# Second product of the second MLP as seven products of half blocks per group, output token-major

## The chip, the cores and the metric

The kernel runs as one program on one core of a Trainium2 chip. The metric is device time in microseconds of one execution. TensorE (PE) multiplies, and its weight loads (PEld) overlap the multiplications; VectorE (DVE) and ScalarE (ACT) work on tiles in SBUF and PSUM; GpSimd (POOL) works on tiles in SBUF; SyncE (SP) issues the DMAs. Each engine takes its own instructions in a fixed order and waits on semaphores.

## The reference

Two residual layers over `x` (1 x 512 tokens x 1024 channels, float32): an attention mixer in the first, an S5 state-space mixer in the second, and behind each of them an MLP. The change is in the second layer's MLP, which ends the program:

```
def sq_relu_mlp(h, w1, w2):
    return jnp.square(jax.nn.relu(h @ w1)) @ w2
...
        x = x + sq_relu_mlp(rms_norm(x, ffn_norm_g[layer]), w_ff1[layer], w_ff2[layer])
```

`w1` is 1024 x 4096 and `w2` is 4096 x 1024. Both products have the same number of multiplications.

## The kernel before

Activations are held channel-major: `xT` is 8 tiles of 128 channels x 512 tokens. Every float32 operand of a large product is split into a rounded high part (type fp32r) and the rest, and one product of two tiles is three matmuls that add up in PSUM: high by high, high by low, low by high (`mm3`, lines 118 to 120 of the profile). A matmul multiplies a 128x128 stationary tile with 512 moving columns.

The class `Mlp` does an MLP in four groups of 1024 hidden channels (`GF` = 8 tiles). In a group, `run` first makes the hidden channels in two halves `c` of four tiles: two weight tiles of 128 x 4 x 512 (`load_w`, L109 the DMA, L112 the high part on ScalarE, L113 the low part on VectorE, in two instructions of 128x1024 each) and 96 matmuls per half. ScalarE and VectorE then take relu and square out of PSUM (L1408, L1409) and split the result into `ahi` and `alo` (L1412, L1413). The group's second product goes over eight output tiles `d`, each with 8 tiles of `w2` as stationary operand and 24 matmuls, so 192 per group. VectorE multiplies the sum in PSUM with the norm's factor `Rb` (L1437) and adds it to `xT` (L1438).

Split weights lie in tiles `whi` and `wlo` of the pool `weights`, which has two buffers of each, for the whole program: a third split can only be written when all matmuls of the first have been done. The raw weights `wraw` have two buffers as well. Sums take turns in six PSUM tiles (`mm6`, names `mm` and `s`). In the last group `emit` writes each finished output tile to HBM, the last one in two halves of 256 tokens.

The order of instructions on each engine comes from a scheduler that runs when the program is built; it keeps the dependencies and may interleave what the code writes one after the other.

Of the kernel before, what the change touches and what calls it, by code (L numbers as in the profile page):

```python
# [9 lines left out]
F32 = mybir.dt.float32  # L10
# [7 lines left out]
P = 128  # L18
S = 512
# [12 lines left out]
def f32(ap):  # L32
    return ap.bitcast(F32)
# [1294 lines left out]
class Mlp:  # L1328
# [38 lines left out]
        T.nc.vector.tensor_scalar(self.Rb, ss, 1.0 / D, EPS, op0=OP.mult, op1=OP.add)  # L1367
        T.nc.vector.reciprocal(self.Rb, self.Rb)

    def run(self, emit=None, during=None, every=0.0, before_last=None, keep=False, halves=False):  # L1370

        T, xT = self.T, self.xT
        nc, tc = T.nc, T.tc
# [4 lines left out]
        with self.ctx if not keep else ExitStack(), tc.tile_pool(name="ffn_a", bufs=1) as pool:  # L1378
# [10 lines left out]
            for g in range(groups):  # L1389
# [30 lines left out]
                for c in range(2):  # L1420
                    W = [T.load_w(self.w2[g * GF * P + kh * 512:g * GF * P + (kh + 1) * 512,
                                          c * 512:(c + 1) * 512]) for kh in range(2)]
                    if last and before_last is not None:
                        with T.behind(nc.sync):
                            before_last(c)
                    for d4 in range(4):
                        d = 4 * c + d4
                        ds_ = slice(d4 * P, (d4 + 1) * P)
                        n = 2 if halves and last and d == KT - 1 else 1
                        for s in (slice(i * S // n, (i + 1) * S // n) for i in range(n)):  # L1430
                            ps = T.mm6()
                            for j in range(GF):
                                hi, lo = W[j // 4]
                                T.mm3(ps[:, s], hi[:, j % 4, ds_], lo[:, j % 4, ds_], ahi[j][:, s], alo[j][:, s],
                                      j == 0, j == GF - 1)

                            ve.tensor_mul(ps[:, s], ps[:, s], self.Rb[:, s])  # L1437
                            ve.tensor_add(xT[:, d, s], xT[:, d, s], ps[:, s])  # L1438
                            pump(5.2 / n)
                            if emit is not None and last:  # L1440
                                emit(d, s)


_INS = ["x", "mix_norm_g", "ffn_norm_g", "w_in", "g_cq", "w_uq", "g_ckv", "w_ukv", "g_qn_mla", "g_kn_mla",
# [11 lines left out]
def trunk(nc, tc, i, out):  # L1456
    with ExitStack() as ctx:
        T = Trunk(tc, ctx)
        gp = T.cpool.tile([P, 31], F32, name="gains")
        T.load_gains = lambda: nc.sync.dma_start(gp, i["gains"])  # L1460
        gmix0, gcq, gckv = gp[:, 0:8], gp[:, 8:10], gp[:, 10:11]
        gains = [gp[:96, 11:12], gp[:96, 12:13], gp[:, 13:14], gp[:, 14:15]]
        gf = gp[:, 15:23], gp[:, 23:31]
        dp = ctx.enter_context(tc.tile_pool(name="dram", bufs=1, space=bass.MemoryType.DRAM))
        T.s5_dram(dp)

        xT, mlp = T.attention(i["xt"], i["w_in"][0], gmix0, gcq, i["w_uq"][0], gckv, i["w_ukv"][0], gains,
                              i["rope"], i["w_o"][0],
                              lambda xT: Mlp(T, xT, gf[0], i["w_ff1"][0], i["w_ff2"][0], "left"))
        mlp.run(emit=lambda d, s: T.s5_emit(xT, d), before_last=lambda c, pool=mlp.pool: T.s5_open(pool, c), keep=True,  # L1470
                during=T.s5_tables(i["s5p"], i["s5b"], i["s5c"], i["s5d"], i["mix_norm_g"][1]), every=6.0)
        mlp = T.s5(xT, i["w_glu"][0],
                   lambda xT: Mlp(T, xT, gf[1], i["w_ff1"][1], i["w_ff2"][1], "right"), mlp.ctx)
        mlp.run(emit=lambda d, s: nc.sync.dma_start(out[d * P:(d + 1) * P, s], xT[:, d, s]), halves=True)


def layout(inputs):
# [24 lines left out]

def unlayout(out):

    return np.ascontiguousarray(out.reshape(D, 8, S // 8).transpose(2, 1, 0)).reshape(1, S, D)


# [14 lines left out]
```

## Time and profile before

| | us |
|---|---|
| median of 3 runs | 1221.34 |
| lowest, highest | 1215.32, 1222.2 |
| profiled execution | 1218.8 |
| its span, first to last instruction | 1217.1 |

The profile shows one execution. Its time beside its span leaves 1.7 us that lie around the instructions. A duration in a row is that of one instruction or of a run of equal ones (x2, x4); instructions of one engine overlap a little at their ends, so the step from one start to the next is shorter than the duration. "Granted clock" is TensorE's clock as a share of 2.4 GHz; 0.5 is 1.2 GHz.

### The profile page before, as it was taken

How to read it: one execution, taken by the hardware profiler on the slowest of the kernel's cores; microseconds unless marked ns; L12 is line 12 of the kernel's file. 1: busy time of each engine (PE TensorE's matmuls, PEld its weight loads, DVE VectorE, ACT ScalarE, POOL GpSimd, SP SyncE). 2: the span in 40 equal slices, each digit the busy share in tenths (PEclk: the TensorE clock that was granted, in tenths of full speed). 3: DMA queues.
4: the chain of work that ended last, by engine and by line, in shares of the span. 5: the costliest groups of instructions: out<-in, count | busy, mean ns of one | idle time of the engine just before them, and what ended most of it. 6: DMA issues, size and time to landing. Idle time of an engine off the chain costs nothing. (4 is left out here: it accounts for less than half of the span.)

```text
span 1217.1 us, 16430 instructions
## 1 busy us (share of the span) xinstructions
PE 1159.6 (95%) x6296; PEld 966.4 (79%) x6296; DVE 782.8 (64%) x1381; ACT 500.6 (41%) x928; POOL 259.6 (21%) x260
## 2 busy tenths in 40 slices
PE   7989999999999888899999788999999999999998
PEld 7978997778888667788888577878788888888887
DVE  7887766758879988797755577453454444444444
ACT  5857775545421433361342255343341331322321
POOL 5461022214000979424200021101000000000000
PEclk9999997999999998999999778999999999999999
DMA  7302202114433376766769677522322332322421
GB/s 222 104 2 53 70 2 69 36 36 160 134 104 103 105 250 190 227 210 198 243 208 394 207 269 256 188 89 85 104 104 70 104 104 69 112 95 69 138 87 52
DMA packets 123758, 161.94 MB, mean 133 GB/s; under 512 B 15648, under 2 KB 72352, under 8 KB 120992
## 3 DMA queue, kind: packets, MB, share of 16 engines
q1 hardware_dynamic: 123680, 160.90, 40.6%
q8 instruction: 49, 0.80, 0.3%
q14 instruction: 29, 0.24, 0.1%
HBM read 133.75 MB, written 35.52 MB: 139 GB/s over the span
## 5 line engine op out<-in xcount | busy, mean ns | idle before, releaser
L112 ACT CAST whi<-wraw 128x1024 fp32r<-128x1024 f32 x132 | 131.9, 1048 | 221.8 <-PE mm L119 123.9
L113 DVE TENSOR_TENSOR wlo<-wraw,whi 128x1024 fp32r<-128x1024 f32 x132 | 169.7, 1315 | 81.1 <-ACT whi L112 80.9
L118 PE MATMUL mm<-xhi,whi 128*128 128x512 f32 x344 | 136.0, 396 | 1.4 <-ACT whi L112 1.4
L118 PE MATMUL mm<-ahi,whi 128*128 128x512 f32 (+1 forms) x352 | 135.0, 386 | 0.3 <-ACT whi L112 0.3
L119 PE MATMUL mm<-xlo,whi 128*128 128x512 f32 x344 | 135.2, 393 | 0.0
L120 PE MATMUL mm<-ahi,wlo 128*128 128x512 f32 (+1 forms) x352 | 134.0, 386 | 1.3 <-DVE wlo L113 1.3
L119 PE MATMUL mm<-alo,whi 128*128 128x512 f32 (+1 forms) x352 | 135.1, 385 | 0.0
L120 PE MATMUL mm<-xhi,wlo 128*128 128x512 f32 x344 | 133.4, 394 | 0.0
L118 PEld LDWEIGHTS mm<-xhi,whi 128*128 128x128 f32 x344 | 64.7, 188 | 16.6 <-ACT whi L112 1.8
L120 PEld LDWEIGHTS mm<-ahi,wlo 128*128 128x128 f32 x352 | 66.1, 188 | 14.7 <-DVE wlo L113 1.7
L118 PEld LDWEIGHTS mm<-ahi,whi 128*128 128x128 f32 x352 | 66.1, 188 | 13.5 <-ACT whi L112 0.6
L119 PEld LDWEIGHTS mm<-alo,whi 128*128 128x128 f32 x352 | 66.2, 188 | 13.1
L120 PEld LDWEIGHTS mm<-xhi,wlo 128*128 128x128 f32 x344 | 64.5, 188 | 14.8 <-issue 0.2
L119 PEld LDWEIGHTS mm<-xlo,whi 128*128 128x128 f32 x344 | 64.7, 188 | 14.4 <-issue 0.2
L1437 DVE TENSOR_TENSOR mm<-mm,bcast 128x512 f32<-128x512 f32 (+1 forms) x44 | 29.8, 684 | 65.4 <-PE mm L120 65.4
L118 PE MATMUL s<-xhi,whi 128*128 128x512 f32 x168 | 66.5, 396 | 0.0
L119 PE MATMUL s<-xlo,whi 128*128 128x512 f32 x168 | 66.5, 396 | 0.0
L120 PE MATMUL s<-ahi,wlo 128*128 128x512 f32 x168 | 66.2, 395 | 0.0
L118 PE MATMUL s<-ahi,whi 128*128 128x512 f32 x168 | 66.1, 395 | 0.0
L120 PE MATMUL s<-xhi,wlo 128*128 128x512 f32 x168 | 66.1, 395 | 0.0
L119 PE MATMUL s<-alo,whi 128*128 128x512 f32 x168 | 65.9, 392 | 0.0
L899 POOL TENSOR_TENSOR W<-PW,B 128x512 f32<-128x512 f32 x16 | 26.4, 1650 | 155.5 <-DVE B L888 141.5
(485 smaller groups left out, 2863.3 us busy)
## 6 DMA issues: line engine op xcount, KB each, us to landing
wraw<-in_w_ff SPq DMA_DIRECT2D x64, 1024.0 KB
dC<-wC SPq DMA_DIRECT2D x16, 512.0 KB
dB<-wB SPq DMA_DIRECT2D x16, 512.0 KB
wraw<-in_w_glu SPq DMA_DIRECT2D x16, 512.0 KB
tT<-dT SPq DMA_DIRECT2D x7, 1024.0 KB
wraw<-in_w_in SPq DMA_DIRECT2D x24, 256.0 KB
tB<-dB SPq DMA_DIRECT2D x6, 1024.0 KB
tC<-dC SPq DMA_DIRECT2D x6, 1024.0 KB
```

Of the source, the lines that this page charges most:

```text
L112: nc.scalar.copy(hi[:, s, :n], raw[:, s, :n])
L113: nc.vector.tensor_sub(lo[:, s, :n], raw[:, s, :n], f32(hi)[:, s, :n])
L118: te.matmul(ps, whi, xhi, start=start, stop=False)
L119: te.matmul(ps, whi, xlo, start=False, stop=False)
L120: self.last = te.matmul(ps, wlo, xhi, start=False, stop=stop).ins
L899: gp.tensor_mul(dst, pw[a][:, :, 1:9, None].to_broadcast(bc), B[a][:, gs][:, :, None, :].to_broadcast(bc))
L1437: ve.tensor_mul(ps[:, s], ps[:, s], self.Rb[:, s])
```

## The change

Only the second MLP changes: `run_seven` takes the place of `run`. Its first product is the same (two halves `c` of 96 matmuls). The hidden channels `p` now hold relu squared times `Rb`, in two VectorE instructions per tile (L1528, L1529 in the changed kernel), and no split of them is made there.

The second product of a group is cut into half blocks. A is 512 tokens x 1024 hidden channels: A11 and A21 are the first and second 256 tokens of the first 512 channels, A12 and A22 of the other 512. B is the group's part of `w2`, 1024 x 1024, in four blocks B11, B12, B21, B22 of 512 x 512. Seven products of 256 x 512 by 512 x 512 take the place of eight, between sums of blocks. On the side of A, VectorE makes S1 = A21 + A22, S2 = S1 - A11, S3 = A11 - A21, S4 = A12 - S2 (L1535, L1541); on the side of B, GpSimd makes T1 = B12 - B11, T2 = B22 - T1, T3 = B22 - B12, T4 = T2 - B21 (L1487). All seven operands of each side are split into high and low parts: those of A by ScalarE and VectorE (L1494, L1495), those of B by ScalarE (L1501) and VectorE, or GpSimd for T1 and T2 (both L1502). The products run in the order B11, T3, T1, T2, T4, B21, B22.

In a product, a 128x128 piece of A is stationary and 512 columns of B move (L1567 to L1569): 24 matmuls for two PSUM tiles of 128 tokens x 512 channels. Each sum over the groups is kept in SBUF (`acc`, two tiles for each of seven products, six of them in the place of `xT`) and added to by VectorE (L1576). The residual `xT` is transposed once by TensorE into four of the sums (L1465). In the last group VectorE combines the seven sums (L1584 to L1590) and the output, now 512 tokens x 1024 channels, is written in nine DMAs, the last two of 128x256.

```diff
+    def run_seven(self, out):
...
+        groups = FF // (GF * P)
+        pairs = [slice(0, 2), slice(2, 4)]
+        with self.ctx, tc.tile_pool(name="ffn_a", bufs=1) as pool:
+            acc = {n: [pool.tile([P, S], F32, name=f"acc{n}{t}") for t in range(2)] for n in (2, 3, 4, 5)}
+            for i, n in enumerate((1, 6, 7)):
+                acc[n] = [xT[:, 2 * i + t] for t in range(2)]
+
+            def residual():
+
+                for n, h, dh in ((5, 1, 1), (3, 0, 1), (2, 0, 0), (4, 1, 0)):
...
+                            pe.transpose(pt[:, k], xT[:, 4 * dh + k, ts], T.ident)
+                        pf = pt.rearrange("p k d -> p (k d)")
+                        if n == 3:
+                            ve.tensor_sub(acc[3][t], pf, acc[5][t])
+                        elif n == 4:
+                            sc.activation(acc[4][t], pf, AF.Copy, scale=-1.0)
+                        else:
+                            sc.copy(acc[n][t], pf)
...
+                for n, fh, dh in (("B11", 0, 0), ("B12", 0, 1), ("B22", 1, 1), ("B21", 1, 0)):
+                    B[n] = pool.tile([P, 4, 512], F32, name=n)
+                    r = (g * GF + 4 * fh) * P
+                    nc.sync.dma_start(B[n], self.w2[r:r + 512, dh * 512:(dh + 1) * 512].rearrange(
+                        "(k p) n -> p k n", p=P))
...
+                B["T3"] = B["B12"]
+                for n, x, y in (("T1", "B12", "B11"), ("T3", "B22", "B12"), ("T2", "B22", "T1"), ("T4", "T2", "B21")):
+                    for s in pairs:
+                        gp.tensor_sub(B[n][:, s], B[x][:, s], B[y][:, s])
+                return B
+
+            def split_a(v):
+                h, l = (pool.tile([P, 4, 256], F32R, name=n, bufs=4) for n in ("ah", "al"))
+                for s in pairs:
+                    x = v(s)
+                    sc.copy(h[:, s], x)
+                    ve.tensor_sub(l[:, s], x, f32(h)[:, s])
+                return h, l
+
+            def split_b(v, eng):
+                hi, lo = T.hi_lo(4)
+                for s in pairs:
+                    sc.copy(hi[:, s], v[:, s])
+                    eng.tensor_sub(lo[:, s], v[:, s], f32(hi)[:, s])
+                return hi, lo
...
+                for c in range(2):
+                    W = self.W0 if g + c == 0 else []
+                    W = W + [self.w1_tile(g, c, kh) for kh in range(len(W), 2)]
+                    if c == 0:
+                        B = sums(g)
...
+                    if g + c == 0:
+                        residual()
+                    for f in range(4):
+                        p = pf[c][:, f]
+                        ve.scalar_tensor_tensor(p, pss[f], 0.0, self.Rb, op0=OP.max, op1=OP.mult)
+                        ve.scalar_tensor_tensor(p, pss[f], 0.0, p, op0=OP.max, op1=OP.mult)
+                    if c == 0:
+                        A["A11"] = split_a(lambda s: a11[:, s])
+
+                        def s3(s):
+                            t = pool.tile([P, 2, 256], F32, name="s3")
+                            ve.tensor_sub(t, a11[:, s], a21[:, s])
+                            return t
+                        A["S3"] = split_a(s3)
...
+                prepare = {
+                    "S1": summed(a21, a21, a22, OP.add),
+                    "S2": summed(a11, a21, a11, OP.subtract),
+                    "A22": lambda s: a22[:, s],
+                    "A12": lambda s: a12[:, s],
+                    "S4": summed(a12, a12, a11, OP.subtract),
+                }
+                order = [(1, "A11", "B11", ve), (7, "S3", "T3", ve), (5, "S1", "T1", gp), (6, "S2", "T2", gp),
+                         (4, "A22", "T4", ve), (2, "A12", "B21", ve), (3, "S4", "B22", ve)]
+                W = {"B11": split_b(B["B11"], ve)}
+                for i, (n, a, b, _) in enumerate(order):
+                    if i < 6:
+                        W[order[i + 1][2]] = split_b(B[order[i + 1][2]], order[i + 1][3])
+                    for _, ahead, _, _ in order[i + 1:i + 3]:
+                        if ahead not in A:
+                            A[ahead] = split_a(prepare[ahead])
+                    (ah, al), (bh, bl) = A[a], W[b]
+                    for t in range(2):
+                        m = 2 if last and i == 6 and t else 1
+                        for cs in (slice(q * S // m, (q + 1) * S // m) for q in range(m)):
+                            ps = T.mm6()[:, cs]
+                            ts = slice(t * P, (t + 1) * P)
+                            for j in range(4):
+                                pe.matmul(ps, ah[:, j, ts], bh[:, j, cs], start=j == 0, stop=False)
+                                pe.matmul(ps, ah[:, j, ts], bl[:, j, cs], start=False, stop=False)
+                                pe.matmul(ps, al[:, j, ts], bh[:, j, cs], start=False, stop=j == 3)
+                            d = acc[n][t][:, cs]
+                            if g == 0 and n in (1, 6, 7):
+                                sc.copy(d, ps)
+                            elif last and n == 4:
+                                ve.tensor_sub(d, d, ps)
+                            else:
+                                ve.tensor_add(d, d, ps)
...
+                    if last and i == 3:
+                        for t in range(2):
+                            a1, a2, a3, a4, a5, a6, a7 = (acc[n][t] for n in range(1, 8))
+                            ve.tensor_add(a6, a1, a6)
+                            ve.tensor_add(a7, a6, a7)
+                            ve.tensor_sub(a4, a7, a4)
+                            ve.tensor_add(a2, a1, a2)
+                            ve.tensor_add(a6, a6, a5)
+                            ve.tensor_add(a3, a6, a3)
+                            ve.tensor_add(a5, a7, a5)
+                            nc.sync.dma_start(out[(2 + t) * P:(3 + t) * P, 512:1024], a5)
...
-        mlp.run(emit=lambda d, s: nc.sync.dma_start(out[d * P:(d + 1) * P, s], xT[:, d, s]), halves=True)
+        mlp.run_seven(out)
...
-    return np.ascontiguousarray(out.reshape(D, 8, S // 8).transpose(2, 1, 0)).reshape(1, S, D)
+    return np.ascontiguousarray(out.reshape(8, S // 8, D).transpose(1, 0, 2)).reshape(1, S, D)
...
-    nc = bacc.Bacc("TRN2", target_bir_lowering=False, num_devices=1)
+    nc = bacc.Bacc("TRN2", target_bir_lowering=False, num_devices=1, dynamic_dma_scratch_size=2048)
...
-    out = nc.dram_tensor("out_0", (D, S), F32, kind="ExternalOutput").ap()
+    out = nc.dram_tensor("out_0", (S, D), F32, kind="ExternalOutput").ap()
```

Three places show how instructions stand now. Row labels of the changed kernel use its own line numbers.

On GpSimd, at the end of the program: the difference of the two orders (T_ is T1, T2 or T4 of a group, B_ a block of `w2`, 8932 to 8934 the first group's, 95.. the second's).

```order
 L1353 TENSOR_TENSOR xacc<-xacc,xsq 128x512 x7
-L1518 UNCONDITIONAL_BRANCH
-L1518 ISA
+L1487 TENSOR_TENSOR T_8932<-B_8926,B_8924 128x1024 x2
+L1487 TENSOR_TENSOR B_8926<-B_8928,B_8926 128x1024
+L1487 TENSOR_TENSOR T_8933<-B_8928,T_8932 128x1024
+L1487 TENSOR_TENSOR B_8926<-B_8928,B_8926 128x1024
+L1487 TENSOR_TENSOR T_8933<-B_8928,T_8932 128x1024
+L1487 TENSOR_TENSOR T_8934<-T_8933,B_8930 128x1024 x2
+L1502 TENSOR_TENSOR wlo<-T_8932,whi 128x1024 x2
+L1487 TENSOR_TENSOR T_9539<-B_9533,B_9531 128x1024 x2
+L1502 TENSOR_TENSOR wlo<-T_8933,whi 128x1024 x2
```

GpSimd had no work in this MLP; now it has twelve instructions of 128x1024 per group, and T1 of the next group (T_9539) stands between the low part of T1 and the low part of T2 of the running one.

On VectorE, before, in the second product of a group:

```order
L113 TENSOR_TENSOR wlo_9864<-wraw_9862,whi_9863 128x1024 x2
L1437 TENSOR_TENSOR mm_9835<-mm_9835,bcast_8393 128x512
L113 TENSOR_TENSOR wlo_9872<-wraw_9870,whi_9871 128x1024
L1438 TENSOR_TENSOR xT_2736<-xT_2736,mm_9835 128x512
L113 TENSOR_TENSOR wlo_9872<-wraw_9870,whi_9871 128x1024
```

The same engine now, in the second group from the second half of T3's low part (al_9811 is the low part of S1, al_9853 of S2, al_9895 of A22; xT holds sums):

```order
L1502 TENSOR_TENSOR wlo_9805<-B12_9533,whi_9804 128x1024
L1529 SCALAR_TENSOR_TENSOR p1_9514<-s_9693,p1_9514 128x512
L1576 TENSOR_TENSOR xT_2736<-xT_2736,s_9818 128x512
L1541 TENSOR_TENSOR p0_9513<-p0_9513 128x2x256
L1495 TENSOR_TENSOR al_9811<-p0_9513,ah_9810 128x512
L1576 TENSOR_TENSOR xT_2736<-xT_2736,mm_9832 128x512
L1541 TENSOR_TENSOR p0_9513<-p0_9513,p1_9514 128x2x256
L1495 TENSOR_TENSOR al_9853<-p0_9513,ah_9852 128x512
L1495 TENSOR_TENSOR al_9895<-p1_9514,ah_9894 128x512 x2
L1541 TENSOR_TENSOR p0_9513<-p0_9513 128x2x256
L1576 TENSOR_TENSOR xT_2736<-xT_2736,mm_9860 128x512
L1495 TENSOR_TENSOR al_9811<-p0_9513,ah_9810 128x512
```

The low part of S1's second half is the last of these rows; seven instructions with both inputs in SBUF stand between it and T3's low part.

On TensorE, before, in the second product of a group:

```order
L120 MATMUL mm_9835<-ahi_9586,wlo_9740 128x512
L118 MATMUL mm_9835<-ahi_9710,whi_9747 128x512
L119 MATMUL mm_9835<-alo_9711,whi_9747 128x512
L120 MATMUL mm_9835<-ahi_9710,wlo_9748 128x512
L118 MATMUL mm_9835<-ahi_9718,whi_9747 128x512
```

The same engine now, in the second group, where the product with T1 (whi_9846) ends and those with T4 (whi_9928) and T2 (whi_9888) go on:

```order
L1569 MATMUL mm_9900<-whi_9846,al_9811 128x512
L1567 MATMUL mm_9900<-whi_9846,ah_9810 128x512
L1568 MATMUL mm_9900<-wlo_9847,ah_9810 128x512
L1569 MATMUL mm_9900<-whi_9846,al_9811 128x512
L1569 MATMUL s_9914<-whi_9846,al_9811 128x512
L1567 MATMUL s_9914<-whi_9846,ah_9810 128x512
L1568 MATMUL s_9914<-wlo_9847,ah_9810 128x512
L1569 MATMUL s_9914<-whi_9846,al_9811 128x512
L1567 MATMUL mm_9982<-whi_9928,ah_9894 128x512
L1567 MATMUL mm_9996<-whi_9928,ah_9894 128x512
L1568 MATMUL s_9940<-wlo_9889,ah_9852 128x512
L1569 MATMUL s_9940<-whi_9888,al_9853 128x512
```

The first of these rows is the 19th matmul of the product with T1 and the first that reads the second half of S1's low part. The products with T2 and T4 are interleaved, and the first matmul with T4 stands right behind the last one with T1, whose buffer T4's high part takes.

## Rows read from the trace of the kernel before

**Rows 1.** The page's first part: busy time, share of the span and instructions by engine

```profile
PE 1159.6 (95%) x6296; PEld 966.4 (79%) x6296; DVE 782.8 (64%) x1381; ACT 500.6 (41%) x928; POOL 259.6 (21%) x260
```

**Rows 2.** Stretches: engines' busy us and count, granted clock, DMA share, GB/s

```profile
core 0: us, PE busy (x) PEld busy (x) DVE busy (x) ACT busy (x) POOL busy (x), PEclk, DMA share, GB/s
860.00:1210.00 350.00, 350.00 (x1531) 285.32 (x1530) 160.38 (x193) 97.27 (x128) 1.30 (x1) 1.00 0.28 93
```

**Rows 3.** Timeline of TensorE in the last group: start us, duration us, instruction

```profile
1205.10 0.39 PE L120 MATMUL mm<-ahi,wlo 128*128 128x512 f32 x1
1205.33 0.39 PE L118 MATMUL mm<-ahi,whi 128*128 128x512 f32 x1
1205.56 0.39 PE L119 MATMUL mm<-alo,whi 128*128 128x512 f32 x1
```

**Rows 4.** Timeline of VectorE at the tail

```profile
1213.52 0.43 DVE L1437 TENSOR_TENSOR mm<-mm,bcast 128x256 f32<-128x256 f32 x1 [1.75 <-PE mm L120]
```

**Rows 5.** Timeline of TensorE: four transposes of 128x128, and the matmul behind them

```profile
514.78 0.63 PE L920 MATMUL pt<-ident,W 128*128 128x128 f32 x4
515.16 0.48 PE L118 MATMUL mm<-xhi,whi 128*128 128x512 f32 x1
```

**Rows 6.** Timeline of ScalarE in the last group

```profile
1147.50 1.99 ACT L112 CAST whi<-wraw 128x1024 fp32r<-128x1024 f32 x2
1149.39 0.62 ACT L1412 CAST ahi<-fp 128x512 fp32r<-128x512 f32 x1
```

**Rows 7.** Timeline of VectorE in the last group, GpSimd idle

```profile
1148.57 2.36 DVE L113 TENSOR_TENSOR wlo<-wraw,whi 128x1024 fp32r<-128x1024 f32 x2
1150.85 1.29 DVE L1413 TENSOR_TENSOR alo<-fp,ahi 128x512 fp32r<-128x512 f32 x2
1152.05 0.68 DVE L1409 SCALAR_TENSOR_TENSOR fp<-mm,fr 128x512 f32<-128x512 f32 x1
```

**Rows 8.** Timeline of GpSimd, VectorE without work of the same kind

```profile
433.81 0.74 POOL L938 TENSOR_TENSOR RT<-RT,rtmp 128x256 f32<-128x256 f32 x1
434.63 0.63 POOL L937 TENSOR_TENSOR rtmp<-E,E 128x256 f32<-128x256 f32 x1
...
512.51 1.29 POOL L901 TENSOR_TENSOR W<-W,t 128x512 f32<-128x512 f32 x1
513.88 1.12 POOL L899 TENSOR_TENSOR t<-PW,B 128x512 f32<-128x512 f32 x1
```

**Rows 9.** Timeline of VectorE in the first MLP, GpSimd busy

```profile
402.22 1.67 DVE L905 TENSOR_TENSOR t<-PW,C 128x576 f32<-128x576 f32 x1
403.81 1.64 DVE L113 TENSOR_TENSOR wlo<-wraw,whi 128x1024 fp32r<-128x1024 f32 x1
```

**Rows 10.** Timeline of GpSimd in the same stretch

```profile
401.18 2.10 POOL L899 TENSOR_TENSOR W<-PW,B 128x512 f32<-128x512 f32 x1
403.24 1.14 POOL L936 TENSOR_TENSOR RT<-E,E 128x256 f32<-128x256 f32 x1
404.34 1.61 POOL L937 TENSOR_TENSOR rtmp<-E,E 128x256 f32<-128x256 f32 x1
```

**Rows 11.** Timeline of VectorE at 515 us, GpSimd waiting

```profile
515.07 0.74 DVE L907 TENSOR_TENSOR CP<-CP,t 128x576 f32<-128x576 f32 x1
515.74 0.74 DVE L916 TENSOR_TENSOR wC<-CP,wC 128x576 fp32r<-128x576 f32 x1
516.41 2.34 DVE L113 TENSOR_TENSOR wlo<-wraw,whi 128x1024 fp32r<-128x1024 f32 x2
```

**Rows 12.** Timeline of GpSimd at 515 us

```profile
515.49 4.24 POOL L899 TENSOR_TENSOR W<-PW,B 128x512 f32<-128x512 f32 x1 [0.48 <-PE pt L920]
```

**Rows 13.** Stretches of the first MLP, columns as in rows 2

```profile
400.00:450.00 50.00, 41.87 (x206) 32.78 (x205) 46.75 (x51) 20.39 (x42) 43.23 (x35) 0.97 0.58 184
...
500.00:550.00 50.00, 50.00 (x261) 41.80 (x260) 40.16 (x59) 22.85 (x44) 19.24 (x12) 1.00 0.69 211
...
412.00:416.00 4.00, 1.70 (x10) 1.07 (x8) 4.00 (x5) 2.14 (x4) 4.00 (x5) 1.00 0.73 241
416.00:420.00 4.00, 3.96 (x19) 3.28 (x20) 4.00 (x4) 1.22 (x4) 4.00 (x4) 0.65 0.41 118
```

More of the change, by code (lines that the diff above doesn't have):

```diff
@@ L1368, in stats, with run @@
         T.nc.vector.reciprocal(self.Rb, self.Rb)
-    def run(self, emit=None, during=None, every=0.0, before_last=None, keep=False, halves=False):
+    def run(self, emit=None, during=None, every=0.0, before_last=None, keep=False):
         T, xT = self.T, self.xT
@@ L1428, in run @@
                         ds_ = slice(d4 * P, (d4 + 1) * P)
[L1429 to L1441, printed above, removed]
+                        ps = T.mm6()
@@ L1469, in trunk @@
                               lambda xT: Mlp(T, xT, gf[0], i["w_ff1"][0], i["w_ff2"][0], "left"))
-        mlp.run(emit=lambda d, s: T.s5_emit(xT, d), before_last=lambda c, pool=mlp.pool: T.s5_open(pool, c), keep=True,
+        mlp.run(emit=lambda d: T.s5_emit(xT, d), before_last=lambda c, pool=mlp.pool: T.s5_open(pool, c), keep=True,
                 during=T.s5_tables(i["s5p"], i["s5b"], i["s5c"], i["s5d"], i["mix_norm_g"][1]), every=6.0)
```

44 lines of the change are left out of this document (added).

## Prediction

> **What bounds the kernel now.** I read the page's first part, then the second MLP by stretches, then single engines on the timeline. TensorE is busy 95% of the span [rows 1]; the reader should then look at the MLP alone: from 860 to 1210 us it is busy for all 350 us at the full clock, while VectorE is busy 160 us, ScalarE 97 us and GpSimd hardly at all, and the DMA engines 28% of the time [rows 2]. So this stage ends when its matmuls have been issued, and its price is their number times their step. The step is not the duration 0.39 us of a row but the distance of two starts: 1205.10 to 1205.33 to 1205.56 [rows 3], 0.227 us on average. All else in the stage has slack, which is what the change spends.
>
> **What it removes.** Per group 168 matmuls of 512 columns stand for 192, in four groups 96 fewer: 96 x 0.227 = 21.8 us. They have the same form, and that w2 moves where activations moved should change nothing in the step. The last multiplication with Rb (0.43 us, two halves of which only the last is on the path) goes from the tail [rows 4]: 0.5 us with its wake-up.
>
> **What it adds to TensorE.** The 32 transposes of the residual: four take 0.38 us up to the next matmul's start [rows 5], so 3.0 us. Without any wait the sum is 1218.8 - 21.8 - 0.5 + 3.0 = 1199.5 us.
>
> **What it adds elsewhere.** Durations of one instruction: on ScalarE 1.0 us for a cast of 128x1024 and 0.6 for 128x512 [rows 6]; on VectorE 1.14 and 0.61 by their steps (2.36 for two, 1.29 for two) [rows 7]. Per group VectorE has 8 + 10 low parts of 128x1024 (w1; five blocks of B), 20.5 us, 22 SBUF instructions of 128x512 for A (14 low parts, 8 sums), 13.4 us, and 30 that read PSUM, 18 us: 52 us in about 82. ScalarE has 8 + 14 casts of 1.0 and 14 of 0.6, about 31 us. By sums both have room. GpSimd has 12 of 128x1024 with two full inputs. No row shows that size; 0.74 us for 128x256 and 1.29 for 128x512 [rows 8] make 1.29 + 512 x 0.00215 = 2.38 us, an estimate; the cheaper row of 1.12 would make it 2.1, and 2.0 to 2.6 are its bounds. That is 29 us per group, also room enough. The eight that make T1 to T4 belong to the next stage and are mostly covered by the first product's 43.6 us. The DMAs add nothing: the same bytes of weights, at 28% of the engines.
>
> **GpSimd and VectorE do not work side by side.** This is the step on which I differ from the sums. From 400 to 405 us VectorE's instructions with two SBUF inputs take 1.67 us (0.74 undisturbed, as in rows 11) and 1.64 (1.14), and GpSimd's between them 2.10 (1.12), 1.14 and 1.61 (0.63 each without): each waits for the other's whole instruction [rows 8 to 10]. At 515 us GpSimd's instruction takes 4.24 us where it needs 1.12, while VectorE's three run undisturbed [rows 11, 12]. The instructions on PSUM are not held up: 0.68 us is their usual price [rows 7]. Where both were 85 to 93% busy, TensorE lost 8 us in 50; with GpSimd at 19 us and VectorE at 40 in 50 it lost none [rows 13]. So it depends on whether the two stand on TensorE's path. Here they do.
>
> **A steady group, from the end of its first product (t = 0).** Undisturbed, product i of 24 matmuls starts at 5.45 x i. GpSimd's first instruction, T1's low part, can start at 6.7: its buffer is free when B11's product ends at 5.45, and a cast of 1.0 us comes first. From there GpSimd has in its order two halves of T1's low part, two of the next group's T1 and two of T2's low part, 6 x 2.38 = 14.3 us. VectorE has, up to T4's low part, 14 SBUF instructions of 128x512 (8.7) and T4's two halves (2.3), 11.0 us. One after the other that is 25.3, to t = 32.0. TensorE wants all of it earlier: S1's low part, second half, at its 19th matmul with T1, t = 15.0; T2's low part at 17.3; T4's at about 20; the block of T2 and T4 undisturbed ends at 27.2. After the last of these operands at least 15 matmuls are left, 3.4 us, so the block ends at 35.4 at the earliest if nothing in the chain idles: 8.2 us late. How late in fact depends on who gets in first.
>
> VectorE first, whenever it has an instruction queued (as at 515 us): GpSimd runs in the gaps, its six at 7.8, 10.8, 15.7, 18.7, 24.2 and 30.1 (gaps are VectorE's reads of PSUM and its waits for ScalarE). S1's second half comes at 18.7, T2's first low half at 26.6 instead of 17.3: 9.3 us late, everything else by then behind it. In turns (as at 400 us): the six start at 7.2, 10.2, 13.2, 16.2, 19.2 and 22.2 with one VectorE instruction between each two; S1's second half comes as the third behind them at 26.4 instead of 15.0, 11.4 late; T4's cast behind it 1.2.
>
> Two waits stand in the order whatever GpSimd does. T4's high part takes the buffer of T1, so the first matmul with T4, which follows the last with T1 directly, waits for a cast, 1.0 us and a wake-up of 0.2 (inside the 9.3 above, but not in the 11.4). B21's low part stands on VectorE behind the sum that reads T4's PSUM tile, so B21's third matmul waits for 0.2 + 0.6 + 1.14 us less its own two steps, 1.6 us. In turns, the gap also costs clock: after a stretch with 1.70 of 4 us busy the next 4 us show 0.65 of the clock [rows 13], of a full gap some 1.7 us. So a group loses 9.3 + 1.6 = 10.9 us in the one case and 11.4 + 1.2 + 1.6 + 1.7 = 15.9 in the other. Queued behind the waiting wlo on GpSimd is only the next group's work; behind VectorE's waiting instructions are the sums that free PSUM, of which six tiles suffice here.
>
> The first three groups have this order. The last has no next T1: 4 x 2.38 + 11.0 and two more sums is 21.7 us from 6.6, so T4's low part at 28.3, ten matmuls behind it 2.3: 30.6 instead of 27.2, and about 1 us for the 12 other sums of the seven products: 4.4.
>
> **Sum.** I take VectorE first, the cheaper of the two, since its instructions follow each other mostly without a gap as at 515 us: 3 x 10.9 + 4.4 = 37.1 us of waits. 1199.5 + 37.1 = 1236.6, say 1237 us. That is against the profiled execution's 1218.8 us; the median is 1221.34, 0.2% above it, and I leave the forecast on the former's scale.
>
> **Rivals.** *In turns:* by the same sum 3 x 15.9 + 4.4 = 52.1, 1252 us. For it speaks the stretch at 400 us, where it holds for many instructions; against it 515 us. The Trainium skill, page "SBUF — State Buffer", section "Who interferes with whom", has a rule of this kind: of a VectorE instruction with two SBUF inputs and a GpSimd one that reads SBUF, the one issued first holds the port for its whole length and the other is fully blocked. By that, the instruction of GpSimd that began at 515.49 should have gone before the two of VectorE that began later, which it did not; the rows at 400 us agree.
>
> *Little contention* (ends not slower): T1's low part runs from 6.7 to 11.5, the next group's T1 from its block's landing at about 12.5 (T3's last reader is done at 5.3; 1 MB at the rate of 93 GB/s for 28% is 3.2 us, and I add the tail's 2 to 4) to 17.3, T2's first low half to 19.6: 2.3 us late, with B21's wait 3.9 per group; the last group 1. 1199.5 + 12.7 = 1212 us. It decides if GpSimd's instructions cost 2 us or less and fall under VectorE's PSUM work. For it speaks the stretch from 500 to 550 us without any loss; there, however, GpSimd's results had no matmul of the MLP waiting.
>
> *No wait at all* (faster): 1199.5 us, if TensorE's order, made for such waits, covers them. The cast of T4 and B21's low part speak against it, which need no contention.
>
> *The gain does not come:* if the step with w2 moving were longer than 0.227, 21.8 us would be gone before any wait, 1258 us. The forms are the same; I give it little.
>
> **Chances.** Forecast 0.45, in turns 0.15, little contention 0.25, none 0.12, no gain 0.03. About 1% is what a measurement of this kernel can tell from no change. Slower by more: most of the forecast's case (1233 and above), all of turns and no gain: 0.56. Within: the rest of the forecast and most of little contention: 0.29. Faster: no wait and a tenth of little contention: 0.15. The range reaches from 1206, between no wait and little contention, to 1255 above turns; it leaves out about 2 in 10, most of it below.
>
> **What would show it.** In the changed profile the steps of matmuls should stay 0.227, and TensorE's idle time should lie in the second half of each group, ended by VectorE's L1495 (S1), GpSimd's L1502 (T2) and L1501, and less in the last group than in the three before. GpSimd's 128x1024 should take 2.4 us in the first product and 3 to 4 in the second; VectorE's L1495 should show means well above 0.69. I am wrong if TensorE shows no gap of several us there, if GpSimd's instructions cost half of my estimate, or if waits stand elsewhere: at the change of groups, for w1 behind the blocks of w2 on SP's queue, or at the first group's transposes.

## The result, and the profile after

The changed kernel takes 1268.18 us (median of 4 runs, 1266.9 to 1268.92) against 1218.62 of the kernel before: a ratio of 1.0405, with a 95% interval of 1.0367 to 1.0443. Forecast were 1237 us and at most 1255.

The page's first part of the changed kernel, beside [rows 1]: TensorE is busy as long as before, 1160 us, though it has 96 matmuls fewer, and the span is 49.4 us longer.

```profile
span 1266.5 us, 16463 instructions
PE 1160.5 (92%) x6220; PEld 961.7 (76%) x6220; DVE 920.8 (73%) x1478; ACT 526.6 (42%) x956; POOL 394.7 (31%) x308
```

The changed kernel by stretches of 50 us, columns as in [rows 2]: where TensorE was busy throughout, it now idles for 6 to 15 us in every second stretch (two of the four are shown), and the granted clock falls in the same ones.

```profile
900.00:950.00 50.00, 34.72 (x138) 27.44 (x139) 41.71 (x36) 19.50 (x29) 23.18 (x9) 0.83 0.14 46
950.00:1000.00 50.00, 48.82 (x211) 39.08 (x210) 31.48 (x29) 14.52 (x17) 17.15 (x6) 1.00 0.31 105
1000.00:1050.00 50.00, 39.41 (x157) 31.11 (x156) 40.90 (x43) 16.64 (x22) 16.65 (x6) 0.87 0.19 64
```

What TensorE waits for in the changed kernel's second MLP (engine, line, releaser: us in total, times, longest):

```profile
PE mm L1569 <- DVE al L1495: 18.2, 2, 9.3
PE s L1569 <- DVE al L1495: 12.4, 2, 7.2
PE pt L1465 <- DVE acc L1468: 6.9, 2, 5.7
PE mm L1567 <- ACT whi L1501: 4.5, 4, 1.7
PE mm L1568 <- DVE wlo L1502: 2.3, 2, 1.1
PE s L1567 <- ACT whi L1501: 1.8, 2, 1.3
PE s L1568 <- DVE wlo L1502: 0.7, 1, 0.7
```

30.6 of 46.8 us are one operand: the second half of S1's low part, waited for once in each group (7.2, 9.3, 8.9 and 5.2 us). 6.9 us lie where no wait had been priced, at the first group's transposes.

How the wait arises stands on the timelines of the second group: VectorE, then GpSimd, then TensorE.

```profile
1024.60 0.68 DVE L1495 TENSOR_TENSOR al<-p,ah 128x512 fp32r<-128x512 f32 x1
1025.80 2.30 DVE L1541 TENSOR_TENSOR p<-p,p 128x512 f32<-128x512 f32 x1
1028.02 8.44 DVE L1495 TENSOR_TENSOR al<-p,ah 128x512 fp32r<-128x512 f32 x3
1036.37 2.83 DVE L1541 TENSOR_TENSOR p<-p 128x512 f32<-128x512 f32 x1
1039.12 0.67 DVE L1576 TENSOR_TENSOR xT<-xT,mm 128x512 f32<-128x512 f32 x1
1039.72 2.23 DVE L1495 TENSOR_TENSOR al<-p,ah 128x512 fp32r<-128x512 f32 x1
```

```profile
1024.67 5.69 POOL L1502 TENSOR_TENSOR wlo<-T,whi 128x1024 fp32r<-128x1024 f32 x2 [36.13 <-DVE p L1541]
1030.44 5.46 POOL L1487 TENSOR_TENSOR T<-B,B 128x1024 f32<-128x1024 f32 x2
1035.87 5.54 POOL L1502 TENSOR_TENSOR wlo<-T,whi 128x1024 fp32r<-128x1024 f32 x2
```

```profile
1032.30 0.39 PE L1567 MATMUL mm<-whi,ah 128*128 128x512 f32 x1
1042.01 0.80 PE L1569 MATMUL mm<-whi,al 128*128 128x512 f32 x1 [9.32 <-DVE al L1495]
1042.60 0.63 PE L1567 MATMUL mm<-whi,ah 128*128 128x512 f32 x1
```

Up to 1025 us VectorE's instruction takes 0.68 us. From GpSimd's first one on, each of VectorE's with two SBUF inputs takes a whole turn, 2.8 us (8.44 for three), GpSimd's six follow each other in 16.7 us without a gap, and there are as many turns as GpSimd has instructions. L1576, which reads PSUM, still takes 0.67. That is the alternation of [rows 9, 10], not the order of [rows 11, 12]. The matmul on the last row stands behind a wait and takes 0.63 instead of 0.39. The granted clock around it (changed kernel, columns as above):

```profile
1032.00:1036.00 4.00, 0.69 (x4) 0.23 (x2) 4.00 (x2) 0.00 (x0) 4.00 (x3) 1.00 0.00 0
1036.00:1040.00 4.00, 0.00 (x0) 0.00 (x0) 4.00 (x4) 0.62 (x1) 4.00 (x2) 0.62 0.00 0
1040.00:1044.00 4.00, 1.99 (x5) 1.61 (x6) 4.00 (x5) 0.00 (x0) 1.40 (x1) 0.50 0.00 0
1044.00:1048.00 4.00, 2.73 (x7) 1.71 (x6) 4.00 (x7) 2.56 (x4) 0.00 (x0) 0.50 0.00 0
1048.00:1052.00 4.00, 4.00 (x13) 3.11 (x12) 2.23 (x3) 0.48 (x1) 0.00 (x0) 0.67 0.02 4
```

TensorE is back at work at 1042 us but runs at 1.2 GHz until about 1050.

The first group's wait has the same cause. VectorE, GpSimd and TensorE of the changed kernel there:

```profile
896.64 2.29 DVE L1495 TENSOR_TENSOR al<-p,ah 128x512 fp32r<-128x512 f32 x1
898.85 2.84 DVE L1495 TENSOR_TENSOR al<-s,ah 128x512 fp32r<-128x512 f32 x1
901.62 2.82 DVE L1495 TENSOR_TENSOR al<-p,ah 128x512 fp32r<-128x512 f32 x1
904.36 0.68 DVE L1468 TENSOR_TENSOR acc<-pt,acc 128x512 f32<-128x512 f32 x1
```

```profile
884.11 4.78 POOL L1487 TENSOR_TENSOR T<-B,B 128x1024 f32<-128x1024 f32 x2 [14.04 <-DMA B<-in_w_ff]
...
898.34 2.81 POOL L1487 TENSOR_TENSOR T<-B,T 128x1024 f32<-128x1024 f32 x1
901.11 5.55 POOL L1487 TENSOR_TENSOR T<-T,B 128x1024 f32<-128x1024 f32 x2
```

```profile
899.00 0.40 PE L119 MATMUL mm<-xlo,whi 128*128 128x512 f32 x1
905.10 1.12 PE L1465 MATMUL pt<-ident,xT 128*128 128x128 f32 x4 [5.70 <-DVE acc L1468]
```

L1468 reads PSUM and is itself not held up (0.68 us), but stands in VectorE's queue behind three that are; the transposes need the PSUM tile that it frees. The row at 884.11, while each of VectorE's instructions has one input in PSUM, also gives GpSimd's undisturbed price: 4.78 us for two, 2.39 each.

### The profile page after: what moved, and what is told of

It is laid out like the page before. It is cut to its first block, busy times and chain, and to the rows that moved or that the text cites. A ratio compares the mean times of both kernels' runs of the same rounds, so it can differ in the third digit from the quotient of the medians.

```text
span 1266.5 us, 16463 instructions
## 1 busy us (share of the span) xinstructions
PE 1160.5 (92%) x6220; PEld 961.7 (76%) x6220; DVE 920.8 (73%) x1478; ACT 526.6 (42%) x956; POOL 394.7 (31%) x308
## 5 line engine op out<-in xcount | busy, mean ns | idle before, releaser
L112 ACT CAST whi<-wraw 128x1024 fp32r<-128x1024 f32 x100 | 99.9, 1048 | 155.8 <-PE mm L119 67.0
L1502 POOL TENSOR_TENSOR wlo<-T,whi 128x1024 fp32r<-128x1024 f32 x16 | 43.9, 2761 | 132.4 <-ACT whi L1501 96.3
L1569 PE MATMUL mm<-whi,al 128*128 128x512 f32 (+1 forms) x156 | 62.6, 404 | 18.2 <-DVE al L1495 18.2
L120 PEld LDWEIGHTS mm<-xhi,wlo 128*128 128x128 f32 x344 | 64.7, 188 | 14.6 <-issue 0.2
L120 PE MATMUL mm<-ahi,wlo 128*128 128x512 f32 x168 | 65.6, 395 | 1.1 <-DVE wlo L113 1.1
L1495 DVE TENSOR_TENSOR al<-p,ah 128x512 fp32r<-128x512 f32 x48 | 66.3, 1412 | 0.0
L119 PE MATMUL mm<-alo,whi 128*128 128x512 f32 x168 | 66.2, 395 | 0.0
L118 PE MATMUL mm<-ahi,whi 128*128 128x512 f32 x168 | 65.9, 396 | 0.0
L1567 PE MATMUL mm<-whi,ah 128*128 128x512 f32 (+1 forms) x156 | 61.2, 404 | 4.6 <-ACT whi L1501 4.5
L1568 PE MATMUL mm<-wlo,ah 128*128 128x512 f32 (+1 forms) x156 | 61.8, 398 | 2.3 <-DVE wlo L1502 2.3
L1501 ACT CAST whi<-B 128x1024 fp32r<-128x1024 f32 x32 | 31.7, 1048 | 63.2 <-PE mm L119 27.4
```

The lines of the kernel that those rows point to most:

```text
L112: nc.scalar.copy(hi[:, s, :n], raw[:, s, :n])
L118: te.matmul(ps, whi, xhi, start=start, stop=False)
L119: te.matmul(ps, whi, xlo, start=False, stop=False)
L120: self.last = te.matmul(ps, wlo, xhi, start=False, stop=stop).ins
L1495: ve.tensor_sub(l[:, s], x, f32(h)[:, s])
L1501: sc.copy(hi[:, s], v[:, s])
```

## The experiments

Theory: VectorE's and GpSimd's instructions with SBUF inputs run in turns, each turn 2.8 us long, so GpSimd's six delay S1's low part. Rival: VectorE's own work or order in the second product is too long, whatever GpSimd does. Behind each expectation stand the run's median time, its ratio to the kernel before and the ratio's 95% interval; a wait list shows the second MLP. In a diff "..." stands for code that is not shown.

**t1_sum_later.** In `sums`, the four sums of a later group are put behind the group's last low part on GpSimd:

```diff
-                        gp.tensor_sub(B[n][:, s], B[x][:, s], B[y][:, s])
+                        with tc.issue_after(lows[-1].ins) if lows else ExitStack():
+                            gp.tensor_sub(B[n][:, s], B[x][:, s], B[y][:, s])
...
```

> The next group's two T1 sums on GpSimd are put behind T2's two low parts, so 4 GpSimd instructions of about 2.75 us instead of 6 stand beside VectorE while it makes S1's low part; nothing else changes. In turns (the engines wait for each other's whole instructions): S1's second half comes up to 2 x 2.75 = 5.5 us earlier in the three groups that have a next one, TensorE's wait there falls from 7.2, 9.3 and 8.9 us to about 2 to 4 us, and the time to about 1250 us. VectorE's own work is too long: GpSimd's order does not matter, 1268 us and the same waits. A late load or T1 sum for the next group: its first products would wait, 1268 us or more.

1251.99 us, ratio 1.0253 [1.0218, 1.0287]. Putting two turns per group off is worth some 16 us. TensorE's waits:

```profile
PE mm L1573 <- DVE al L1497: 12.7, 3, 7.1
PE s L1573 <- DVE al L1497: 8.1, 2, 5.1
PE pt L1466 <- DVE acc L1469: 6.8, 2, 5.6
PE mm L1571 <- ACT whi L1503: 5.7, 3, 4.2
```

The waits for low parts of A fell from 30.6 to 20.8 us, and what the products lose beside their waits from 14.6 to 12.5. That refutes the rival as the whole cause: VectorE's work and order stayed. S1's wait came to the 2 to 4 us expected in the first and third groups (2.9 and 2.3 us); in the second 7.1 are left, since there the sums that were put off begin at 1036.65 us, before S1's second half is made, and take turns with VectorE all the same.

**low_on_vector.** GpSimd out of the second product's way:

```diff
-... (5, "S1", "T1", gp), (6, "S2", "T2", gp),
+... (5, "S1", "T1", ve), (6, "S2", "T2", ve),
...
-                        gp.tensor_sub(B[n][:, s], B[x][:, s], B[y][:, s])
+                        if g and n == "T1" and not s.start:
+                            marks.append(gp.tensor_copy(mark, f32(A["S4"][1])[:, 0, 0:1]))
+                        with tc.issue_after(marks[-1].ins) if marks else ExitStack():
+                            gp.tensor_sub(B[n][:, s], B[x][:, s], B[y][:, s])
```

> T1's and T2's low parts go from GpSimd to VectorE (4 instructions of about 1.21 us more for it in each group), and the next group's T1 sums wait, by a small copy on GpSimd, until VectorE has made S4's low part, so that GpSimd does nothing while S1, S2, A22, A12 and S4 are prepared. In turns: S1's second half is late by about 1 us a group instead of 5 to 9, the clock keeps 2.4 GHz there, the first group's wait at the transposes (6.9 us) stays: about 1235 us. VectorE's own work is too long: 4.8 us more of it in each group, 1278 to 1287 us.

1223.45 us, 1.0025 [1.0006, 1.0043]: 45 us less than the changed kernel, some 12 below what the theory expected, although VectorE has 4.8 us more to do per group. TensorE's waits:

```profile
PE pt L1467 <- DVE acc L1470: 6.9, 2, 5.6
PE mm L1573 <- DVE wlo L1507: 1.6, 4, 0.8
PE s L1574 <- DVE al L1500: 0.5, 1, 0.5
PE s L1573 <- DVE wlo L1507: 0.4, 1, 0.4
```

Of 39.9 us of waits in the seven products 2.5 are left. The edit also changed what it did not aim at: in the built programs of this run, t1_sum_later and s1_first the scheduler has put most of T4's product behind T2's on TensorE. S1's wait stands ahead of all but two of these products' matmuls; the 6.3 us for ScalarE's casts in the changed kernel's list may in part be due to that order.

**residual_by_scalar.**

```diff
-                            ve.tensor_sub(acc[3][t], pf, acc[5][t])
+                            sc.copy(acc[3][t], pf)
...
+                for t in range(2):
+                    ve.tensor_sub(acc[3][t], acc[3][t], acc[5][t])
```

> The first group's two subtractions out of PSUM on VectorE become copies by ScalarE, with the subtraction made later in SBUF, so that the transposes' PSUM buffer no longer waits for VectorE. In turns with the wait at the transposes as a loss of its own: 6.9 us and some 2 us of clock go, 1259 us. In turns, but the time only moves to the next thing that VectorE owes (S1's low part in the same group, now 7.2 us): 1264 to 1268 us. VectorE's own work is too long: the same, 1268 us.

1262.3 us, 1.0345 [1.0314, 1.0375], between the two. The 6.9 us became 4.5, now for ScalarE's copy of another transposed block, which stood in ScalarE's queue behind the cast of S3's second half, and so behind VectorE's turns (row of ScalarE):

```profile
906.02 0.62 ACT L1496 CAST ah<-s 128x512 fp32r<-128x512 f32 x1 [8.99 <-DVE s L1537]
```

**no_gpsimd.** T1 to T4 replaced by B11, B22, B12 and B21 in `order`, GpSimd's sums removed, `ve` for all low parts.

> Leaves out the sums of w2's blocks: B11, B12, B21 and B22 stand in the place of T1 to T4, so the output is not the reference's; the low parts all go to VectorE, and GpSimd does nothing in the second MLP. Matmuls, transposes and all else are as in the changed kernel. In turns: the waits for S1 and at the transposes go, with the clock that they cost, and about 1205 to 1218 us are left (the matmuls' sum without waits was 1199.5 us, and the waits for ScalarE's casts are some 5 us). VectorE's own work is too long: waits of 5 us and more a group stay, 1235 us or more. The saving of matmuls does not come: over 1225 us with few waits on TensorE.

1224.86 us, 1.0043 [1.0016, 1.007]: above the 1205 to 1218 expected. No wait at the transposes any more, but 12.4 us in the seven products, for ScalarE's casts and VectorE's low parts of B; with the clock behind them these products are 23.6 us above their steps. Most of this comes from a fault in the edit. B21 now stands twice in a row in `order`, and its second split replaces the first in `W` before the product in T4's place has read it. In the built program no matmul reads the first split, and that product waits for the second one, which is made a place later. In the second group VectorE begins T1's low part 8.9 us after the seven products begin and T2's after 16.5, as in low_on_vector; the low part that the product in T4's place reads is begun after 26.5 us, T4's in low_on_vector after 21.8. So this run shows that the waits for S1 and at the transposes go with GpSimd's work; its time says nothing on the rival. VectorE is busy without a pause from 1000 to 1025 us here, but so it is in low_on_vector, where 2.5 us of waits are left.

**gpsimd_halves.** The same work of GpSimd in pieces of 128x512:

```diff
-                    for s in pairs:
+                    for s in [slice(k, k + 1) for k in range(4)]:
                         gp.tensor_sub(B[n][:, s], B[x][:, s], B[y][:, s])
```

and L1502 alike where the engine is GpSimd.

> All of GpSimd's sums and low parts in pieces of 128x512 instead of 128x1024, twice as many; the work is the same. In turns: a VectorE instruction waits for one piece of about 1.4 us instead of 2.75, so VectorE's 128x512 steps beside GpSimd take about 1.5 us instead of 2.8, S1's second half comes some 6 us earlier a group, and the wait there falls to 1 to 4 us; GpSimd gets no more turns than VectorE, so T2's low part comes later and takes back a part, 1250 to 1262 us. A port shared by rate, whatever the pieces' size: VectorE's steps stay near 2.8 us, 1268 us.

1252.14 us, 1.0267 [1.0241, 1.0292]. VectorE and GpSimd, second group:

```profile
1019.40 5.19 DVE L1495 TENSOR_TENSOR al<-p,ah 128x512 fp32r<-128x512 f32 x3
```

```profile
1017.16 6.87 POOL L1503 TENSOR_TENSOR wlo<-T,whi 128x512 fp32r<-128x512 f32 x4 [34.43 <-DVE p L1544]
```

A turn is 1.73 us instead of 2.8: its length follows the size of GpSimd's instruction. A port shared by rate would have left 2.8. TensorE's waits for S1's low part fell from 30.6 to 13.4 us, and 19.7 us for ScalarE's casts took part of the gain back.

**s1_first.** VectorE's order alone:

```diff
-                            A[ahead] = split_a(prepare[ahead])
+                            with tc.issue_after(s1_low[-1].ins) if ahead in ("S2", "A22") else ExitStack():
+                                A[ahead] = split_a(prepare[ahead])
```

> The changed kernel with VectorE's order alone changed: both halves of S1's sum and low part come before S2's and A22's; GpSimd keeps its instructions. In turns: S1 is prepared in 4 instructions fewer that each wait for 2.75 us of GpSimd, the wait there falls from 5 to 9 us to about 1, but S2's and T2's low parts are then late by 3 to 5 us a group: about 1250 us. If VectorE's order were the whole cause: the waits of S1 go and none takes their place, 1235 us or less.

1246.34 us, 1.0214 [1.0181, 1.0247]. S1's wait is gone from three groups (3.9 us once), others took its place:

```profile
PE mm L1569 <- ACT whi L1502: 6.9, 3, 3.8
PE pt L1466 <- DVE acc L1469: 6.9, 2, 5.6
PE s L1569 <- ACT whi L1502: 4.3, 2, 3.8
PE mm L1570 <- DVE wlo L1503: 4.0, 1, 4.0
```

Another order on VectorE alone is worth 22 us, getting out of GpSimd's way 45: the order is part of how the turns come to bear on S1, not the whole cause.

**What low_on_vector still lost.** By the terms (1218.8 - 21.8 + 3.6 for transposes + 2.5 + 6.9 and some 3 us of clock) it should have taken 1213 us. Of the missing 10 us 2.8 lie upstream of the change and 1.9 in the tail (the end of the program behind the last matmul); 4.5 are a step of 0.2333 us instead of 0.2267 in the seven products. The new tile `mark`, 4 bytes a partition, had moved the operands behind it by 32 bytes. Two runs on this: low_on_vector_64 makes `mark` 64 bytes, and before_x64 puts an unused tile of 32 bytes ahead of the second MLP's x in the kernel before:

```diff
+        if side == "right":
+            self.ctx.enter_context(T.tc.tile_pool(name="pad", bufs=1, side=side)).tile([P, 8], F32, name="pad")
         self.pool = pool = self.ctx.enter_context(T.tc.tile_pool(name="ffn", bufs=1, side=side))
```

> The same as low_on_vector, with the little tile that its small copy writes made 64 bytes a partition instead of 4, so that all operands of the seven products start at multiples of 64 bytes in a partition again, as in the changed kernel, and no longer at 32 past one. If the start decides TensorE's step (560 cycles against 544 of 2.4 GHz in low_on_vector): the 684 matmuls step by 0.227 us instead of 0.233, 4 x 1.1 us less, about 1219 us, or a little more where the casts are waited for instead. If it was something else in low_on_vector (VectorE's low parts beside the matmuls): 0.233 stays, 1223.5 us.

> The kernel before, with an unused tile of 32 bytes a partition ahead of the second MLP's x, so that xhi and xlo there start at multiples of 64 bytes instead of 32 past one; nothing else changes. If the start decides TensorE's step: the first products' 768 matmuls step by 0.227 us as the second products' do, 768 x 0.0065 = 5.0 us less, about 1214.5 us. If not: 1219.5 us, and 0.2333 us stays there.

low_on_vector_64: 1223.07 us, 1.0030 [1.0009, 1.0050], step 0.2333: multiples of 64 do not decide. before_x64: 1213.4 us, 0.9952 [0.9932, 0.9972], step 0.2267: the start does decide something.

**Remainders.** `mark` of 128 bytes; an unused tile of 96 bytes instead of 32 in the kernel before; the same and 64 bytes at the front of SBUF; `mark` of 256 bytes (in all_together_256, below); and an unused tile of 128 bytes ahead of the activations `ahi`, `alo` of both MLPs.

> The same as low_on_vector with the little tile of 128 bytes, so that the seven products' stationary operands start at the same remainder of 128 as the moving ones (64, as in the changed kernel); with 64 bytes they stood at 0 against 64 and stepped by 0.2333 us, with 4 bytes at 96 against 64. If the two remainders of 128 decide: 0.2267 us comes back, 4.5 us less than low_on_vector, about 1219 us. If VectorE's making the low parts slows the matmuls: 0.2333 us stays, 1223 us.

> The kernel before with an unused tile of 96 bytes ahead of the second MLP's x: its moving operands start at 0 past a multiple of 128 in a partition, the weights, which stand still, at 64. If a start at a multiple of 64 is all that counts: 0.2267 us a matmul and 1213.5 us, as in before_x64. If the two must agree in their remainder of 128, or if 64 is the fast remainder for each: 0.2333 us and 1219 us.

> before_x0 with one more tile of 64 bytes at the front of SBUF, so that the weights and the operands of all large products start at 0 past a multiple of 128, moving and standing alike. If the two must agree: 0.2267 us a matmul and 1213.5 us. If 64 is the fast remainder for each: 0.2333 us in all of the MLPs' products, some 1224 us.

> The kernel before with an unused tile of 128 bytes ahead of the activations of both MLPs' second products, so that these start at 64 past a multiple of 256 and the weights still at 192. If the remainders of 256 must agree: these 2 x 768 matmuls step by 0.2333 us instead of 0.2267, 10 us more, about 1229 us. If not: 1219 us.

1220.5 (1.0011 [0.9988, 1.0033]), 1221.18 (1.0012 [0.9990, 1.0033]), 1218.55 (1.0000 [0.9976, 1.0024]) and 1228.76 us (1.0068 [1.0046, 1.0091]). The first three refuted both readings by 128 and left one that fits all rows, the remainder of 256; all_together_256 and before_a128 tested it. Starts are those of the built programs, modulo 256 bytes in a partition; steps are means over a product on the timeline, waits and gaps in the records left out (standing is the stationary operand, moving the one of 512 columns):

| kernel, product | standing | moving | step us |
|---|---|---|---|
| before, first | 192 | 224 | 0.2333 |
| before, second | 192 | 192 | 0.2268 |
| changed, seven | 192 | 192 | 0.2267 |
| low_on_vector, seven | 224 | 192 | 0.2333 |
| low_on_vector_64, seven | 0 | 192 | 0.2333 |
| low_on_vector_128, seven | 64 | 192 | 0.2333 |
| all_together_256, seven | 192 | 192 | 0.2267 |
| before_x64, first | 192 | 192 | 0.2267 |
| before_x0, first | 192 | 128 | 0.2333 |
| before_all0, first | 0 | 128 | 0.2333 |
| before_all0, second | 0 | 0 | 0.2268 |
| before_a128, second | 192 | 64 | 0.2333 |

Rows of the kernel before (first product) and of before_a128 and before_x64, the first and the last of four starts each: three steps take 0.70, 0.70 and 0.68 us.

```profile
959.81 0.40 PE L118 MATMUL s<-xhi,whi 128*128 128x512 f32 x1
...
960.51 0.39 PE L118 MATMUL s<-xhi,whi 128*128 128x512 f32 x1
```

```profile
1004.96 0.39 PE L118 MATMUL s<-ahi,whi 128*128 128x512 f32 x1
...
1005.66 0.40 PE L120 MATMUL mm<-ahi,wlo 128*128 128x512 f32 x1
```

```profile
960.24 0.39 PE L118 MATMUL mm<-xhi,whi 128*128 128x512 f32 x1
...
960.92 0.39 PE L118 MATMUL s<-xhi,whi 128*128 128x512 f32 x1
```

**The parts together.** all_together is low_on_vector_64 with x as in before_x64 and, in the first group, L1468 ahead of A11's low part:

```diff
-                        A["A11"] = split_a(lambda s: a11[:, s])
+                        with ExitStack() if g else tc.issue_after(got[-1].ins):
+                            A["A11"] = split_a(lambda s: a11[:, s])
```

all_together_128 and _256 enlarge `mark` and put S3's split behind ScalarE's last copy in the same way.

> low_on_vector_64 with two more edits: VectorE subtracts the first group's two transposed residuals before A11's and S3's low parts, and the second MLP's x starts at multiples of 64 bytes as in before_x64. In turns with each loss its own: 6.9 us of waiting at the transposes and about 2 us of clock go, and 5.0 us of the first products' steps: 1219 - 9 - 5 = 1205 us. If the second product is bound by VectorE's work: little beyond the 5 us, 1213 us.

> all_together with the little tile of 128 bytes, and in the first group S3's cast and low part behind ScalarE's copies of the transposes, for which TensorE still waited 5.0 us there. In turns with each loss its own: 5.0 us of waiting, some 2 us of clock, and 4.5 us of the seven products' steps go from 1212.2: about 1201 us. If the time only moves to the next wait in the first group: 1207 us.

> all_together_128 with the little tile of 256 bytes. With it the seven products' stationary and moving operands start at the same remainder of 256 bytes in a partition (192), as every operand pair has had that stepped by 0.2267 us a matmul so far; all pairs that stepped by 0.2333 us differed in it. If that decides: 0.2267 us in the seven products, 684 x 0.0065 = 4.5 us less, about 1205.5 us. If the making of low parts on VectorE slows them: 0.2333 us and 1210 us.

1212.16 (0.9956 [0.9935, 0.9978]), 1209.92 (0.9920 [0.9892, 0.9949]) and 1204.29 us (0.9887 [0.9856, 0.9919]). The first missed its 1205: 5.0 us of waiting for ScalarE's copy had taken the place of VectorE's, and the step had stayed 0.2333. The second removed that wait and missed 1201 by the step, which the third brought back. What is left of all_together_256's waits are six short ones for VectorE's low parts, 4.1 us together and at most 1.0 each.

Part of its gain is not the change's: before_x64 has the same start of x and is 0.9952. Between these two, from the matmul ahead of the reciprocal to the last matmul, the changed products save 10.9 us (326.6 against 337.5), where the sum without waits has some 18. Of the difference 4.1 us are the waits; the other 3 are not attributed.

## Why the prediction was wrong

The step that failed is "I take VectorE first, the cheaper of the two". In turns was named, with the right mechanism, and got 0.15 and 1252 us; it too is 16 us short, for the terms below that neither sum had. The point by which I chose, that VectorE's instructions follow each other without a gap as at 515 us, holds here too and does not give VectorE precedence. Why GpSimd's instruction waited there through several [rows 11, 12] was not tried. The Trainium skill, page "SBUF — State Buffer", section "Who interferes with whom", has the lock for a whole instruction, taken by the one issued first. The 2.8 us turns, and 1.73 with half the size, agree with the lock; the rows at 515 us do not agree with its order.

Term by term, against the profiled execution's 1268.2 us:

- Matmuls removed: 21.8 us as predicted; the step with w2 moving is 0.2267 us.
- Transposes: 3.0 predicted; 3.6 by the first product of all_together_256, which waits for nothing, against before_x64's (36.0 and 32.4 us).
- The seven products in four groups: 37.1 us of loss predicted, 52.1 in turns; measured 54.5. They last 51.7, 54.4, 53.3 and 47.5 us from their first matmul to the next product's, against 168 x 0.2268 = 38.1. Of this 39.9 us are waits in the list; in turns made them 47.0. S1's second half came at t = 24.4 (1041.9 less 1017.5) where the forecast said 18.7 and in turns 26.4, since a turn is 2.8 us and not 2.38 + 0.61.
- The other 14.6 us are mostly clock (10.7 us by the matmuls that step by 0.26 to 0.44 us), mis-sized in both sums: 1.7 us a group in turns, none in the forecast. I read one stretch of 4 us from [rows 13]; here TensorE ran at half clock for some 7 us of the second group after its gap, with the wait for T4's cast, 1.3 us, in between.
- The last group: 4.4 us predicted, 9.4 measured, by the same turns: its wait for S1 is 5.2 us.
- The first group's transposes: nothing priced, 6.9 us and 2.3 of clock. It was named only as a place where I could be wrong. The cost of GpSimd's sums was called covered by the first product; what I had not followed is who else queues on VectorE behind the instructions that they hold up.
- Tail: 0.5 us less predicted; 4.4 us from the last matmul's start to the end instead of 3.9.
- GpSimd's 128x1024: 2.38 us estimated, 2.39 undisturbed.
- Upstream: VectorE's reciprocal starts at 877.86 instead of 873.99, 3.9 us later; among these runs it starts between 870.3 (s1_first) and 880.0 (t1_sum_later), in code that neither touches, so this term lies within the scatter.

1218.8 - 21.8 + 3.6 + 54.5 + 9.2 + 3.9 = 1268.2; with the tail's 0.5 it would be 1268.7. The share that experiments undo: turns 45 us at least with their clock (low_on_vector), in spite of 4.5 us lost to the step there; the transposes' wait goes in all_together_128. That the rest of low_on_vector's gain would fail to appear for the operands' starts, no theory of mine had.

## What to carry to other kernels

Ahead of giving GpSimd a share of VectorE's work, count the instructions of GpSimd that stand between VectorE and the operand that TensorE waits for: each cost one whole turn here. Follow also what queues behind VectorE's held instructions, reads of PSUM among them. A saving of matmuls is only worth what the engines that prepare their operands leave of it; after a gap, add the time at half clock. When a tile is added anywhere in SBUF, look at the matmuls' step afterwards, not at waits alone.

## What the runs showed of the hardware

- A large fp32r matmul (128x128 standing, 512 columns moving) steps by 0.2267 us where the standing and the moving operand start at the same remainder of 256 bytes in a partition, and by 0.2333 where they do not: 16 cycles of 2.4 GHz. Twelve products of ten kernels fit, the slow ones 32, 64 or 128 bytes apart; one of the kernel before's two products had paid it, and 32 unused bytes make that kernel 0.5% faster (0.9952 [0.9932, 0.9972]). Only matmuls of this shape were compared, and why it is so isn't shown.
- Turns between VectorE and GpSimd last one instruction of each: 2.8 us with 128x1024 on GpSimd and 128x512 on VectorE, 1.73 with 128x512 on both, while VectorE's instructions with one input in PSUM keep their 0.68.
